# Row dot products of an expert layer on VectorE alone, without the share that GpSimd and ScalarE took

## The chip, the cores and the metric

One core of one Trainium2 chip runs one program. The metric is the device time of a run in microseconds (us), as the median of three runs. The engines are TensorE (PE for its matmuls, PEld for its weight loads), VectorE (DVE), ScalarE (ACT), GpSimd (POOL) and SyncE (SP). TensorE's granted clock is shown as a share of 2.4 GHz, so 0.50 is its lower level of 1.2 GHz.

## The reference, cut to what matters

One layer over 1024 tokens plus 16 meta tokens, width 1024: a mixer with two branches of eight heads each, and then an expert layer (`peer_ffn`) that picks 16 of 16384 experts per head and token, so 128 experts for each token:

```python
def one_block(xb):
    ...
    idx = jnp.take_along_axis(i1, ci // TOPK, axis=-1) * N_KEYS \
        + jnp.take_along_axis(i2, ci % TOPK, axis=-1)
    gate_w = jax.nn.softmax(sc, axis=-1)
    act = jax.nn.gelu(jnp.einsum('thkd,td->thk', expert_u[idx], xb).astype(jnp.float32),
                      approximate=False)
    coef = (gate_w * act).astype(xb.dtype)
    return jnp.einsum('thk,thkd->td', coef, expert_v[idx])
```

All arrays are float32. The change touches the first `einsum`: the dot product of a gathered row of `expert_u` with the token's own vector.

## The kernel before, in words

The tokens are eight blocks of 128. They go through the mixer in three groups of 2, 3 and 3 blocks (`GROUPS`, function `mixer`): projections and both branches head by head, then `branches`, `merge` and `rank` (query projection and scores), and `route`, which finds the 128 experts of each token on VectorE.

The expert layer is done in two ways. The first five blocks gather (`experts`): for each block, 128 indirect DMAs, issued on GpSimd's queue, each bring one row of `expert_u` of 1024 floats for each of the 128 tokens, 512 KB in all, into a buffer `G`. `G` has eight slots (`NG`). The list `out` holds the rows that are on their way, and `use` takes them from its head. A row of kind "u" is multiplied with the block's normalised tokens (`h2p`) and summed over the 1024 columns, which gives one column of `ac`. There are two ways to do this. Either VectorE does both in one `scalar_tensor_tensor` with `accum_out`, or GpSimd multiplies in place, the row becomes kind "a" and stays at the head of `out`, and ScalarE sums it by a copy with `accum_out`. After a block's 128 dots, 128 more gathers bring rows of `expert_v` (kind "v"), which TensorE weighs and sums in the PSUM tile `pv`. So there are 640 rows of u and 640 of v. The last three blocks go a dense way (`dense`): TensorE computes all 16384 experts for them, first with `u_t` (tile `ua`), then with `expert_v` (tile `acc`). The gathers of the first five blocks run beside the mixer of groups 1 and 2 and beside the dense part.

All instructions are put in order by a planner before the kernel is built. `Clock` keeps a planned time for each engine; `Engine` adds each instruction's estimated duration; `Weave` always takes the next piece from the generator whose planned time is earliest. The planner's estimates are 1.195 us for a fused dot on VectorE (`dve_time`: (1024 + 123) / 960), 2.28 us for the multiplication on GpSimd (`pool_time`) and 1.07 us for the sum on ScalarE (`act_time`). It has no term for two engines that hinder each other. Within an engine the order is fixed when the kernel runs. Some small choices hang on the planned clocks too: `scale` and `copy` take ScalarE or VectorE, whichever is planned to be free first, and in group 0 the split of weights (tile `wlo`) takes GpSimd or VectorE (line 397).

Which way a row's dot goes is chosen in `use`, where `DS2` is 0:

```python
if x.kind == "u" and clk.t["pool"] + 1.2 < clk.t["dve"] + DSL + max(0.0, min(DSM, DS2 * (clk.t["dve"] - clk.t["dma"]))):
    pool.tensor_tensor(x.G, x.G, x.h2, op=OP.mult)
    x.kind = "a"
    return
if x.kind == "a":
    act.activation(x.G, x.G, AF.Copy, accum_out=x.ac[:, x.j:x.j + 1])
elif x.kind == "u":
    dve.scalar_tensor_tensor(x.G, x.G, 1.0, x.h2, op0=OP.mult, op1=OP.mult,
                             accum_out=x.ac[:, x.j:x.j + 1])
```

How many rows the plan wants gathered by when is set by `bias`: in the mixers it grows when the planned DMA clock falls behind those of TensorE and VectorE, and in the dense part it ties the share of rows left to the share of weight chunks left.

Of the kernel before, what the change touches and what calls it, by code (L numbers as in the profile page):

```python
# [36 lines left out]
CB = 4  # L37
KB = 50
RW = 2
DSL = -2  # L40
PSL = 1
ASL = 0
NDENSE = 3
# [229 lines left out]
def _build(ctx, tc, nc, a, groups, dbg, peer):  # L273
# [1014 lines left out]
    def use(x):  # L1288

        if x.kind == "u" and clk.t["pool"] + 1.2 < clk.t["dve"] + DSL + max(0.0, min(DSM, DS2 * (clk.t["dve"] - clk.t["dma"]))):  # L1290
            pool.tensor_tensor(x.G, x.G, x.h2, op=OP.mult)
# [326 lines left out]
```

## Time and profile before

| what | before |
|---|---|
| median of 3 runs | 4220.03 us (4211.74 to 4225.68) |
| profiled execution, its own time | 4197.44 us |
| its span, first to last instruction | 4195.7 us |
| mean granted clock of TensorE | 0.962 |
| PE busy | 3811.1 us (91%) |
| VectorE busy | 2771.6 us (66%) |
| ScalarE busy | 1749.3 us (42%) |
| GpSimd busy | 1862.4 us (44%) |

Busy time is the time in which an engine shows an instruction; an instruction that starts and is then held up counts as busy for as long as it lasts. Shares are means over the whole span. Stage by stage: the mixer of group 0 until about 560 us, then its merge and rank; the gathers from 633 us on; the mixer of group 1 until about 1640, of group 2 until about 2780; the dense part with `u_t` until 3534, and with `expert_v` from 3553 to 4179.

### The profile page before, as it was taken

The numbers are of one execution on the slowest core, as the hardware profiler recorded it, in microseconds if no ns is written. First come the engines' busy times: TensorE is split into PE (matmuls) and PEld (weight loads), VectorE is DVE, ScalarE is ACT, GpSimd is POOL, SyncE is SP. The second block draws the span as 40 slices with busy tenths as digits, with TensorE's granted clock in tenths as the row PEclk, the third lists the DMA queues.
The fourth block names the chain that finished last, engine by engine and source line by source line (L and its number), as shares of the span: only waits on it lengthen the run. The fifth ranks groups of instructions, "written<-read, shape, count | busy, mean of one in ns | idle before, by whom it ended". The sixth has DMA issues, their size and how long they took to land. (4 is left out here: it accounts for less than half of the span.)

```text
span 4195.7 us, 62111 instructions
## 1 busy us (share of the span) xinstructions
PE 3811.1 (91%) x20086; PEld 2750.6 (66%) x20086; DVE 2771.6 (66%) x8155; ACT 1749.3 (42%) x4336; POOL 1862.4 (44%) x1633
## 2 busy tenths in 40 slices
PE   6999988998999978999999989779989898999998
PEld 5777875665445766455555557568888797766665
DVE  5555469998863658888876536669868464744444
ACT  4566443444331232344333312236648573333332
POOL 3222444445553545565656635443434243433332
PEclk9999999999999989999999999899999999999999
DMA  3332368786898988999889989888888888999996
GB/s 105 91 96 87 114 205 268 257 295 233 314 351 288 346 320 294 323 331 335 319 305 337 349 278 347 302 286 275 292 267 296 297 292 296 349 328 333 328 329 221
DMA packets 525911, 1162.17 MB, mean 277 GB/s; under 512 B 55376, under 2 KB 262000, under 8 KB 525200
## 3 DMA queue, kind: packets, MB, share of 16 engines
q0 software_dynamic: 186960, 679.04, 45.5%
q1 hardware_dynamic: 303328, 459.04, 32.9%
q10 hardware_dynamic: 35296, 20.12, 1.6%
q8 instruction: 158, 2.59, 0.3%
q14 instruction: 169, 1.38, 0.1%
HBM read 1082.32 MB, written 75.66 MB: 276 GB/s over the span
## 5 line engine op out<-in xcount | busy, mean ns | idle before, releaser
L185 POOL DMA_INDIRECT G<-in_expert_v_dram,idxT x640 | 737.0, 1152 | 1070.6 <-PE pv L185 482.1
L185 POOL DMA_INDIRECT G<-in_expert_u_dram,idx x640 | 724.5, 1132 | 733.2 <-DVE G L185 247.1
L185 DVE TENSOR_TENSOR wlo<-wraw,whi 128x512 fp32r<-128x512 f32 (+2 forms) x644 | 543.8, 851 | 725.2 <-ACT whi L185 688.5
L185 ACT CAST whi<-wraw 128x512 fp32r<-128x512 f32 (+2 forms) x816 | 527.6, 659 | 577.7 <-PE prj L185 201.6
L185 DVE SCALAR_TENSOR_TENSOR G<-G,h2p 128x1024 f32<-128x1024 f32 x574 | 710.6, 1241 | 11.2 <-DMA G<-in_expert_u_dram,idx 11.2
L185 PE MATMUL ua<-hD,whi 128*128 128x384 f32 x2048 | 542.1, 346 | 31.7 <-ACT whi L185 31.6
L185 PE MATMUL prj<-hW,wraw 128*128 128x384 f32 x1280 | 476.3, 506 | 18.4 <-ACT junk L185 7.2
L185 PEld LDWEIGHTS ua<-hD,whi 128*128 128x128 f32 x2048 | 367.7, 191 | 70.5 <-ACT whi L185 36.8
L185 POOL TENSOR_TENSOR wlo<-wraw,whi 128x384 fp32r<-128x384 f32 (+1 forms) x172 | 202.6, 1186 | 401.0 <-ACT whi L185 344.5
L185 PE MATMUL prj<-wraw,hW 128*128 128x512 f32 x768 | 378.0, 606 | 0.0
L185 PE MATMUL pv<-G,Zb 128*32 128x512 f32 x2560 | 365.0, 621 | 14.1 <-DMA G<-in_expert_v_dram,idxT 14.0
L185 PE MATMUL ua<-hD,wlo 128*128 128x384 f32 x1024 | 350.4, 342 | 10.9 <-DVE wlo L185 9.9
L185 PEld LDWEIGHTS prj<-hW,wraw 128*128 128x128 f32 x1280 | 234.8, 197 | 165.0 <-issue 29.0
L185 PE MATMUL acc<-whi,Chi 128*128 128x512 f32 x768 | 309.3, 403 | 17.3 <-ACT whi L185 17.0
L185 PE MATMUL acc<-wlo,Chi 128*128 128x512 f32 x768 | 300.0, 391 | 0.5 <-DVE wlo L185 0.5
L185 PE MATMUL acc<-whi,Clo 128*128 128x512 f32 x768 | 300.0, 391 | 0.0
L185 PEld LDWEIGHTS acc<-whi,Chi 128*128 128x128 f32 x768 | 144.4, 188 | 110.8 <-issue 63.7
L185 PEld LDWEIGHTS ua<-hD,wlo 128*128 128x128 f32 x1024 | 195.0, 190 | 17.2 <-DVE wlo L185 17.0
L185 PE MATMUL prj<-oTs,whi 128*128 128x384 f32 (+1 forms) x768 | 186.3, 330 | 19.0 <-DVE oTs L185 9.8
L185 PEld LDWEIGHTS prj<-wraw,hW 128*128 128x128 f32 x768 | 131.1, 194 | 90.1 <-issue 84.8
L185 ACT CAST Chi<-Gr 128x384 fp32r<-128x384 f32 x125 | 64.1, 513 | 264.6 <-DVE Gr L185 211.2
L185 PEld LDWEIGHTS acc<-whi,Clo 128*128 128x128 f32 x768 | 144.5, 188 | 31.5 <-DVE Clo L185 0.3
(326 smaller groups left out, 7241.1 us busy)
## 6 DMA issues: line engine op xcount, KB each, us to landing
wraw<-in_u_t_dram SPq DMA_DIRECT2D x256, 256.0 KB, 4.8
wraw<-in_expert_v_dram SPq DMA_DIRECT2D x128, 512.0 KB, 5.4
wraw<-in_w_b_dram SPq DMA_DIRECT2D x192, 256.0 KB, 4.8
wraw<-in_w_a_dram SPq DMA_DIRECT2D x192, 192.0 KB, 3.9
wraw<-in_w_q_dram SPq DMA_DIRECT2D x96, 256.0 KB, 5.9
gscr<-Gl SPq DMA_DIRECT2D x125, 192.0 KB, 4.7
Gr<-gscr SPq DMA_DIRECT2D x125, 192.0 KB
wraw<-in_w_g_dram SPq DMA_DIRECT2D x96, 192.0 KB, 6.0
```

What stands on the lines that cost most here:

```text
L185: return f(*a, **k)
```

## The change

One constant in the rule of `use` changes. With -2 the GpSimd way is taken when GpSimd's planned clock lies more than 3.2 us behind VectorE's; with -1000 it would have to lie more than 1001.2 us behind.

```diff
@@ -37,7 +37,7 @@
 CB = 4
 KB = 50
 RW = 2
-DSL = -2
+DSL = -1000
 PSL = 1
 ASL = 0
 NDENSE = 3
```

## Rows read from the trace of the kernel before

**Rows 1.** The page, part 1: busy time of each engine over the span.

```profile
PE 3811.1 (91%) x20086; PEld 2750.6 (66%) x20086; DVE 2771.6 (66%) x8155; ACT 1749.3 (42%) x4336; POOL 1862.4 (44%) x1633
```

**Rows 2.** Windows: length; busy of PE, PEld, DVE, ACT, POOL; clock; DMA share; GB/s.

```profile
633.00:3670.00 3037.00, 2755.51 (x14069) 1929.33 (x14068) 2175.04 (x6600) 1252.73 (x3096) 1479.18 (x1241) 0.96 0.87 305
633.00:1050.00 417.00, 379.45 (x1708) 237.24 (x1707) 376.21 (x1217) 177.94 (x538) 202.25 (x164) 0.96 0.78 263
1420.00:1640.00 220.00, 178.38 (x929) 140.15 (x930) 147.01 (x361) 69.48 (x122) 109.74 (x89) 0.90 0.89 317
2460.00:2790.00 330.00, 273.54 (x1405) 208.59 (x1404) 203.71 (x508) 92.03 (x158) 160.25 (x139) 0.91 0.88 309
3670.00:4196.00 526.00, 508.48 (x2431) 352.74 (x2429) 244.17 (x433) 157.27 (x204) 165.83 (x150) 0.99 0.89 308
...
3700.00:4100.00 400.00, 399.68 (x1917) 276.03 (x1916) 190.66 (x340) 125.23 (x163) 140.04 (x127) 1.00 0.95 328
```

**Rows 3.** The chain that ended last, from 4130 us: start, length, what.

```profile
4134.93 7.90 DMA G<-in_expert_v_dram,idxT
...
4143.94 33.60 PE acc L185 x147
```

**Rows 4.** Tile G: count, min/median/max ns of one, first and last start.

```profile
L185 POOL DMA_INDIRECT G<-in_expert_u_dram,idx x640: 932/940/4291, 633.0 to 3640.6; - x160
...
L185 DVE SCALAR_TENSOR_TENSOR G<-G,h2p x574: 1154/1218/14726, 644.2 to 3654.4; 128x1024 f32<-128x1024 f32 x192
L185 DVE DVE_READ_ACCUMULATOR G<-G,h2p x574: 70/83/97, 645.4 to 3655.6; 128x1 f32 x192
L185 POOL TENSOR_TENSOR G<-G,h2p x66: 2327/2374/2704, 645.0 to 3660.6; 128x1024 f32<-128x1024 f32 x66
L185 ACT ACTIVATE G<-G x66: 1040/1056/1080, 647.7 to 3665.1; 128x1024 f32<-128x1024 f32 x66
L185 ACT ACTIVATION_READ_ACCUMULATOR G<-G x66: 182/187/215, 648.7 to 3666.1; 128x1 f32 x66
```

**Rows 5.** VectorE's timeline near 645, 982 and 3662 us.

```profile
645.38 2.77 DVE L185 TENSOR_TENSOR hit<-iota_c,posf 128x400 f32<-128x400 f32 x1
648.18 0.58 DVE L185 TENSOR_TENSOR hit<-hit,cand 128x400 f32<-128x400 f32 x1
...
981.93 14.73 DVE L185 SCALAR_TENSOR_TENSOR G<-G,h2p 128x1024 f32<-128x1024 f32 x1
...
3661.62 2.46 DVE L185 TENSOR_TENSOR wlo<-wraw,whi 128x1024 fp32r<-128x1024 f32 x1 [3.11 <-ACT whi L185]
...
3667.23 1.23 DVE L185 TENSOR_TENSOR wlo<-wraw,whi 128x1024 fp32r<-128x1024 f32 x1 [1.44 <-ACT whi L185]
```

**Rows 6.** GpSimd's timeline near 982 us.

```profile
981.74 13.83 POOL L185 TENSOR_TENSOR G<-G,h2p 128x1024 f32<-128x1024 f32 x6
```

**Rows 7.** TensorE's timeline near 982 us; in brackets the idle time before it.

```profile
997.38 0.79 PE L185 MATMUL bg<-vtok,Y 128*128 128x128 f32 x2 [12.51 <-ACT X L185]
```

**Rows 8.** Windows over 42 held-up VectorE instructions, each to 2 us past it; their sum.

```profile
sum 197.00, PE 149.54 PEld 114.19 DVE 181.39 ACT 97.63 POOL 122.49; mean PE 3.56 PEld 2.72 DVE 4.32 ACT 2.32 POOL 2.92
```

**Rows 9.** Windows, columns as in Rows 2: a stretch full of fused dots, and after 989.7 us.

```profile
941.00:981.00 40.00, 38.53 (x184) 23.78 (x183) 37.42 (x129) 18.09 (x55) 24.61 (x19) 1.00 0.82 271
...
989.70:1003.40 13.70, 6.02 (x11) 3.54 (x12) 13.32 (x41) 4.51 (x10) 6.49 (x4) 0.50 0.23 72
```

**Rows 10.** Tile h2p from 633 to 1050 us, columns as in Rows 4.

```profile
L185 DVE SCALAR_TENSOR_TENSOR G<-G,h2p x122: 1201/1217/14726, 644.2 to 1048.7; 128x1024 f32<-128x1024 f32 x122
...
L185 POOL TENSOR_TENSOR G<-G,h2p x14: 2327/2354/2704, 645.0 to 993.2; 128x1024 f32<-128x1024 f32 x14
```

**Rows 11.** Waits of all engines: us in total, times, longest.

```profile
POOL G L185 <- ACT G L185: 352.7, 53, 44.4
```

**Rows 12.** Waits of TensorE's matmuls, columns as in Rows 11.

```profile
PE pv L185 <- DMA G<-in_expert_v_dram,idxT: 14.0, 11, 2.7
```

**Rows 13.** Windows of tile idxT: VectorE, GpSimd (gathers of v); clock, DMA, GB/s.

```profile
3670.00:4196.00 526.00, 0.29 (x1) 159.16 (x138) 0.99 0.89 308
```

## The prediction

> **What bounds the kernel now.** I read the busy times first. TensorE is busy for 3811.1 of 4195.7 us, no other engine for more than 66% [rows 1], and the work that ended last is a run of 147 matmuls of the dense part, with two output blocks behind it [rows 3]. The change alters no matmul. So the time can move only by the 384.6 us in which TensorE is idle, by stretches in which it is granted its lower clock, and by whatever would make the last stage wait.
>
> Next I asked where this idle time lies. The 66 rows that go the GpSimd way fall between 645 and 3661 us [rows 4], and in 633 to 3670 TensorE is idle for 3037 - 2755.5 = 281.5 us [rows 2]. In the last stretch that is full of gathers, 3700 to 4100, it is idle for 0.3 us [rows 2]: there is nothing to win there, and only something to lose.
>
> Then I looked at what VectorE does while GpSimd multiplies. From 981.74 us GpSimd runs six multiplications in 13.83 us [rows 6]. A fused dot of VectorE that started 0.19 us after them took 14.73 us [rows 5], where 1.218 us is usual [rows 4]. It came out as GpSimd was done. The same is seen with others: a comparison of 128x400 took 2.77 us beside the multiplication at 645.0, and its neighbour of that size 0.58 us; a weight split took 2.46 us beside the last multiplication, and the next one 1.23 us [rows 5]. In all, 42 VectorE instructions that overlap one of the 66 multiplications last over 0.5 us longer than the median of their own form (the pairs shown are the first and the last of these 42). Their surplus adds up to 99.9 us. So a multiplication on GpSimd doesn't take work off VectorE here: it holds VectorE up for 99.9 / 66 = 1.51 us on average, and a fused dot with its accumulator read would cost 1.218 + 0.083 = 1.30 us [rows 4].
>
> TensorE feels it. In the windows over these 42 instructions it is idle for 197.0 - 149.5 = 47.5 us [rows 8], 24% of them; elsewhere in 633 to 3670 it is idle for (281.5 - 47.5) / (3037 - 197) = 8.2%. Beyond that share, 47.5 - 0.082 x 197 = 31.3 us of idle time lie beside held-up instructions. The largest piece is the 12.51 us before 997.38, which ends as the fused dot comes free and ScalarE and TensorE get their input [rows 7].
>
> **The change, part by part.** All sums are against the profiled execution's 4197.4 us.
>
> *Multiplications removed from GpSimd.* 66 x 2.374 = 157 us of GpSimd go. GpSimd's own time is not on the path (44% busy [rows 1]); what counts is VectorE's 99.9 us of hold-up. What is that worth to TensorE? At least the one gap whose cause can be followed instruction by instruction, 12.5 us; at most the whole surplus, 31.3 us. Some of the rest would be there anyway, because the planner takes the GpSimd way just when VectorE is late. I take the middle, -22.
>
> *Clock.* After the long gap TensorE worked at half its clock from 989.7 to 1003.4 us, with 6.0 us of matmuls in it [rows 9], which would take 3.0 at the full clock. The other gaps beside the held-up instructions are under 5 us. Between 0 and -6; I take -4.
>
> *Fused dots added to VectorE.* 66 x 1.30 = 86 us, against 99.9 us that go: VectorE's busy time should fall by some 14 us. The price for TensorE lies between nothing and the rate that the hold-ups show, 31.3 / 99.9 = 0.31 us for each us of delay, so 27 us. The nearest row is a stretch where VectorE is 94% busy, mostly with fused dots: 941 to 981, where TensorE is idle for 1.5 of 40 us [rows 9], 3.7%. A dot of 1.3 us fits between the planned uses; a hold-up of 2.7 us less often does. 0.037 x 86 = 3; I take +3 and keep 27 for the range.
>
> *Sums removed from ScalarE.* 66 x (1.056 + 0.187) = 82 us of 1749 [rows 1, 4]. It is 42% busy, so nothing to -5; I take 0.
>
> *Gathers.* GpSimd stands for 352.7 us before gathers whose slot ScalarE's sum frees [rows 11], and these waits go; others of the same kind behind VectorE's dots take part of their place. TensorE, however, waits for gathered rows for only 14.0 us in all [rows 12]: 0 to -14, and I take -3.
>
> By a rule of the Trainium skill the price would be larger. The page "SBUF — State Buffer", section "Who interferes with whom", says that a VectorE instruction with two SBUF inputs and a GpSimd instruction that reads SBUF exclude each other, and that whichever comes second waits until the first is done. If every multiplication met such an instruction, VectorE would lose 66 x 2.374 = 157 us instead of 99.9, and the gain from the hold-up would be 157 / 99.9 of mine, -35 instead of -22. The trace decides: some multiplications meet nothing that they hold up.
>
> *The order.* The planner counts 1.195 us more on VectorE for each of the 66 rows, 79 us in all, 0 on GpSimd and ScalarE, and will weave everything after 645 us differently; `scale` and `copy` will take ScalarE somewhat more often. What such a reshuffle can do is seen from the two tails of the mixer, which do the same work for three blocks: 220 - 178.4 = 41.6 us idle in one, 330 - 273.5 = 56.5 in the other [rows 2]. I take 0, with 15 us to either side.
>
> Sum: -22 - 4 + 3 + 0 - 3 + 0 = -26 us, so 4171 for a profiled execution like this one. That execution lies 22.6 us under the median of the runs, 4220.0. I take the same difference from the median: 4194 us, 0.6% faster. About 0.3%, 12.7 us, is what a measurement of this kernel can tell from no change.
>
> **The rivals.**
>
> *Nothing to measure.* If TensorE's idle time beside the hold-ups was there for other reasons, only the long gap and its clock come back, -12.5 - 3; and if the dots cost half of their upper rate, 13 us go again: -2.5, so 4217. For it: the multiplications stand where VectorE is late by plan, which means stage changes, where TensorE has gaps anyway. Against it: 24% idle beside 8.2%.
>
> *Too much left for the end (slower).* If the dots are planned 79 us later, rows slip by 79 / (3037 / 640) = 17, and as v follows u, 17 of u and 17 of v move past 3670 us, where 138 rows of v are gathered now [rows 13]. A row is 0.524 MB, at 328 GB/s [rows 2] 1.6 us. DMA is 95% busy in 3700 to 4100, which leaves 20 us: enough for 13 rows. 34 rows would need 54 us, so TensorE would wait for 34 us: 4254. It decides from 13 rows on. Against it: in the mixers the plan's bias calls rows by DMA's lag, and DMA rather than VectorE is nearly full there, 0.88 to 0.89 in the tails [rows 2].
>
> *A full engine gets fuller (slower).* From 633 to 1050 VectorE is busy for 376 of 417 us [rows 2], and 14 of the 66 rows lie there [rows 10]. If VectorE's queue sets that stretch's end, 14 x 1.30 = 18 us are added, and if the hold-ups there fell into time that it had, nothing comes back: 4238. The Trainium skill, "Perfetto Trace Analysis", section "Optimizing Scalar/DVE Operations", says that with a saturated VectorE it may pay to move work to other engines, GpSimd too; the same paragraph warns that these two share a read port. Against it: 13.5 us of the stretch are the one held-up dot itself, more than half of the 18.
>
> That the change does nothing can be ruled out: GpSimd's planned clock would have to lie 1001 us behind VectorE's, but each gather moves it on, and the gathers wait for slots that VectorE frees.
>
> **How the numbers follow.** Forecast (-26; its own range -13 to -45, so 4175 to 4207) 0.5; nothing to measure 0.3; too much left 0.12; fuller engine 0.08. The forecast splits into 0.45 faster and 0.05 within 0.3%; the second case 0.05 faster, 0.24 same and 0.01 slower; the last two 0.02 same and 0.18 slower. Together 0.50, 0.31, 0.19. The low end takes all the terms' best: -31 - 6 + 0 - 5 - 14 - 15 = -71, about 4150. The high end must take in most of the slower cases: 4242.
>
> **What would show it.** Right: 640 fused dots near 1.22 us and none of over 3; no multiplication of `G` on GpSimd; VectorE busy for some 14 us less, ScalarE for 82 less and GpSimd for about 157 less; no gap of TensorE like that before 997; TensorE's idle time in 633 to 3670 down from 281 to about 255. Wrong: idle time of TensorE after 3670 us, with rows of u there; or VectorE over 95% busy in the stretch after 633 with TensorE's idle time up. If the idle time beside the hold-ups is gone and the total is the same, the order took it back elsewhere.

## The result and the profile after

The changed kernel takes 4165.9 us (4151.5 to 4172.0, four runs) against 4222.0 us for the kernel before beside it: a ratio of 0.9872, 95% interval 0.9848 to 0.9896. Timed once more, with the last experiments, it gave 0.9878 (0.9860 to 0.9895). So it is 1.2 to 1.3% faster, some 51 to 54 us. The forecast was 4194 us, 0.6% or 26 us faster, with a range of 4150 to 4242: the direction holds and the range holds the time, but the gain is twice the forecast.

A reading aid for all that follows: the trace of before that the prediction rests on came from an execution that ran 22.6 us under its median. A second trace of the same kernel, taken with the first experiment, has a span of 4209.7 us. Where times are compared, the ratios to before on the same chip are used, and a difference of ratios is turned into us with 4210. The experiments ran on three chips, and after itself ran again on only one of them, with the last four; "slower than after" takes its ratio there, 0.9878, for all, and each such difference has some 10 us to either side.

The page of the changed kernel, part 1, busy time of each engine over its span of 4170.3 us:

```profile
PE 3808.9 (91%) x20086; PEld 2761.5 (66%) x20086; DVE 2746.6 (66%) x8282; ACT 1684.7 (40%) x4209; POOL 1720.4 (41%) x1567
```

Against [rows 1], VectorE has 25 us less, ScalarE 65, GpSimd 142. VectorE does 66 more dots and is busy for less time. ScalarE's fall is less than the 82 us of its sums.

Its tile `G`, count, min/median/max ns, first and last start, and the same windows as in [rows 2] (length; busy of PE, PEld, DVE, ACT, POOL; clock; DMA share; GB/s):

```profile
L185 DVE SCALAR_TENSOR_TENSOR G<-G,h2p x640: 1199/1218/1285, 646.0 to 3632.3; 128x1024 f32<-128x1024 f32 x160
L185 DVE DVE_READ_ACCUMULATOR G<-G,h2p x640: 70/83/93, 647.1 to 3633.4; 128x1 f32 x160
```

```profile
633.00:3670.00 3037.00, 2776.38 (x14168) 1953.75 (x14167) 2159.48 (x6746) 1194.31 (x2976) 1319.77 (x1183) 0.96 0.88 308
633.00:1050.00 417.00, 388.15 (x1742) 240.55 (x1740) 370.79 (x1278) 165.85 (x517) 181.82 (x157) 0.97 0.83 274
...
3700.00:4100.00 400.00, 400.00 (x1919) 276.30 (x1919) 193.07 (x341) 125.90 (x162) 161.46 (x122) 1.00 0.96 333
```

All 640 dots are on VectorE, at the same median as in [rows 4], and the longest takes 1.285 us instead of 14.7. TensorE is idle for 3037 - 2776.4 = 260.6 us in 633 to 3670, where it was 281.5 [rows 2], or 288.8 in the second trace of before. In 633 to 1050 it is idle for 28.9 us instead of 37.6. In 3700 to 4100 it is not idle at all.

The waits for slots have moved, not gone. In the waits of all engines (us in total, times, longest), the row of ScalarE in [rows 11] is missing. The row of VectorE in before, and those of VectorE and TensorE in after, are:

```profile
POOL G L185 <- DVE G L185: 450.6, 167, 41.6
```

```profile
POOL G L185 <- DVE G L185: 708.0, 184, 44.4
POOL G L185 <- PE pv L185: 591.0, 183, 56.6
```

In before GpSimd stood for 450.6 us behind VectorE's dots and for 352.7 behind ScalarE's sums, 803 in all; now it is 708 behind the dots alone. What a large wait is worth can't be read from its own size.

### The profile page after: what moved, and what is told of

The parts are those of the page before. It is cut to its first block, busy times and chain, and to the rows that moved or that the text cites. A ratio compares the mean times of both kernels' runs of the same rounds, so it can differ in the third digit from the quotient of the medians.

```text
span 4170.3 us, 62056 instructions
## 1 busy us (share of the span) xinstructions
PE 3808.9 (91%) x20086; PEld 2761.5 (66%) x20086; DVE 2746.6 (66%) x8282; ACT 1684.7 (40%) x4209; POOL 1720.4 (41%) x1567
## 5 line engine op out<-in xcount | busy, mean ns | idle before, releaser
L185 POOL DMA_INDIRECT G<-in_expert_v_dram,idxT x640 | 755.2, 1180 | 1128.7 <-PE pv L185 536.4
L185 DVE TENSOR_TENSOR wlo<-wraw,whi 128x512 fp32r<-128x512 f32 (+2 forms) x644 | 513.3, 803 | 720.3 <-ACT whi L185 666.7
L185 DVE SCALAR_TENSOR_TENSOR G<-G,h2p 128x1024 f32<-128x1024 f32 x640 | 776.6, 1217 | 14.3 <-DMA G<-in_expert_u_dram,idx 12.9
L185 PEld LDWEIGHTS prj<-oTs,whi 128*128 128x128 f32 x768 | 137.8, 198 | 40.1 <-issue 11.9
```

The lines of the kernel that those rows point to most:

```text
L185: return f(*a, **k)
```

## The experiments

The question was which part of the change gives the gain: that GpSimd's multiplications no longer hold VectorE up, that GpSimd's queue is shorter, that ScalarE is free of the sums, or only that the planner wove another order. Each ratio below is to before on the same chip, with its 95% interval.

**Before once more.**

```diff
(no edit)
```

> The kernel before, unchanged, timed against itself and traced a second time. Every theory expects a ratio within 0.3% of 1. The question is what one trace of this kernel is worth: the first trace of before ran 22 us under its median, and the two traces differ by 25 us where the runs differ by 56. If the trace shows a span near 4220 us, the missing 30 us will be seen in its stages; the 12.5 us gap of TensorE before 997 us should stand in it again if it belongs to the order of the instructions.

Measured: 1.0006 (0.9989 to 1.0023), so the comparison can see some 0.2%. The gap is there again. TensorE's and VectorE's timelines of this trace:

```profile
995.61 0.79 PE L185 MATMUL bg<-vtok,Y 128*128 128x128 f32 x2 [12.44 <-ACT X L185]
```

```profile
980.23 14.66 DVE L185 SCALAR_TENSOR_TENSOR G<-G,h2p 128x1024 f32<-128x1024 f32 x1
```

The held-up dot lasts 14.66 us and the gap 12.44, where the first trace has 14.73 and 12.51 [rows 5, 7]. In this trace 45 instructions beside the 66 multiplications are held up, by 111.4 us (42 and 99.9 in the first). The hold-ups repeat; they are no accident of one execution.

**Before's order, dots on VectorE.** The planner is told what it was told in before; the instructions that come out differ.

```diff
 if x.kind == "u" and clk.t["pool"] + 1.2 < ...:
+    pool.swap = lambda *a, **k: nc.vector.scalar_tensor_tensor(
+        x.G, x.G, 1.0, x.h2, op0=OP.mult, op1=OP.mult, accum_out=x.ac[:, x.j:x.j + 1])
     pool.tensor_tensor(x.G, x.G, x.h2, op=OP.mult)
+    pool.swap = None
...
 if x.kind == "a":
+    act.swap = lambda *a, **k: None
     act.activation(x.G, x.G, AF.Copy, accum_out=x.ac[:, x.j:x.j + 1])
+    act.swap = None
```

> The planner sees before's program, so the order on TensorE is that of before, instruction by instruction; only the 66 multiplications on GpSimd and the 66 sums on ScalarE are left out, and 66 fused dots stand on VectorE at the places of the multiplications. Hold-up theory (GpSimd's multiplications held VectorE up): most of the gain comes without a new order, 30 to 56 us faster than before, ratio 0.987 to 0.993. Order theory (the gain is the new order that the planner wove): within 0.3% of before, or slower by the 86 us of dots times up to 0.31, ratio 0.997 to 1.006.

Measured: 0.9904 (0.9878 to 0.9931), 40 us faster, 29 to 51. TensorE runs the same instructions in the same order as in before. No VectorE instruction beside a gathered row is held up any more, and the gap before 997 us is gone, although the six dots that replace the six multiplications stand on VectorE there. The window of 633 to 3670:

```profile
633.00:3670.00 3037.00, 2782.72 (x14232) 1946.58 (x14232) 2167.30 (x6760) 1199.59 (x2977) 1329.85 (x1185) 0.96 0.88 309
```

TensorE is idle for 254.3 us here. The order theory falls as an account of the whole: most of the gain comes without a new order. The run takes three things away at once, the hold-up, GpSimd's time and ScalarE's sums, and adds the dots; the runs after it add one thing at a time.

Three more rows of this trace: the waits of GpSimd and of TensorE's matmuls, and the stretch where the matmuls now stand that had the gap before them in before.

```profile
POOL G L185 <- DVE G L1291: 350.0, 43, 46.9
PE pv L185 <- DMA G<-in_expert_v_dram,idxT: 14.2, 11, 2.5
```

```profile
975.00:989.00 14.00, 12.63 (x53) 8.20 (x52) 13.59 (x61) 5.12 (x15) 0.00 (x0) 1.00 0.51 168
```

The gathers wait behind the moved dots (L1291) for as long as they did behind ScalarE's sums, 350.0 us where it was 352.7 [rows 11], and the kernel is 40 us faster: the gain doesn't come from shorter waits for slots. TensorE's wait for gathered rows hasn't changed either, 14.2 us and 14.0 [rows 12], though 157 us of GpSimd's time are gone. And TensorE has its full clock in that stretch.

As the order is the same, this trace and the second one of before can be laid beside each other matmul by matmul. From 633 to 1123 us, where 16 of the 66 rows lie and 29 us of hold-up go, this one gains 17 us; from 1692 to 2927, with 18 rows and 23 us of hold-up, it gains 1; from 2927 to 3215, with 12 rows and 23 us, 11. (Against the first trace of before it is 20, 0 and 11; the two traces of before differ from each other by up to 8 us in a single stretch.) So what the exchange is worth depends on the place. Why it is worth nothing in the middle isn't shown.

**GpSimd's multiplications put back as extra work.** After's program; the 66 rows are the ones that before gave to GpSimd (`AT` lists them by block and number, here and in the runs below). The row's buffer is dead at this point, so this adds nothing to the result.

```diff
 elif x.kind == "u":
     dve.scalar_tensor_tensor(x.G, x.G, 1.0, x.h2, ...)
+    if (x.b, x.j) in AT:
+        nc.gpsimd.tensor_tensor(x.G, x.G, x.h2, op=OP.mult)
```

> After's program and order, and behind the dots of the same 66 rows as in before GpSimd multiplies the row's buffer, which nobody reads any more, with the tokens (66 times 2.4 us of GpSimd that add nothing to the result). Hold-up theory: VectorE is held up by about 1.5 us for each, 100 us in all, and the time goes back by 20 to 45 us, ratio to before 0.992 to 0.998; VectorE's instructions of more than twice their usual time are back in the trace. Order theory: 0.987, as after, since the order is after's.

Measured: 1.0050 (1.0032 to 1.0067): not only the gain goes, it is slower than before. Against after that is 72 us for 66 multiplications, more than the 20 to 45 expected. 56 VectorE instructions are held up, by 113.9 us. VectorE's and GpSimd's timelines near 1520 us:

```profile
1520.14 3.48 DVE L186 TENSOR_TENSOR wlo<-wraw,whi 128x512 fp32r<-128x512 f32 x1 [0.28 <-ACT whi L186]
1523.54 1.21 DVE L186 SCALAR_TENSOR_TENSOR G<-G,h2p 128x1024 f32<-128x1024 f32 x1
```

```profile
1520.68 2.38 POOL L1301 TENSOR_TENSOR G<-G,h2p 128x1024 f32<-128x1024 f32 x1
1523.21 1.24 POOL L186 DMA_INDIRECT G<-in_expert_u_dram,idx  x1 [0.16 <-issue]
```

A weight split that takes 0.69 us elsewhere takes 3.48: by these rows it starts half a microsecond before the multiplication, and ends half a microsecond after it.

**Memsets in place of the multiplications.**

```diff
+    if (x.b, x.j) in AT:
+        for n in range(3):
+            nc.gpsimd.memset(x.G[:, :900], 0.0)
```

> As the run with the added multiplications, at the same 66 places, with three memsets of 900 columns in place of each, about as long on GpSimd but reading nothing (the values that they leave are not used). If it is reading by GpSimd that holds VectorE up: as after, ratio to before 0.985 to 0.990, and no held-up instruction. If it is GpSimd's time or its later gathers that cost: the same as with the added multiplications, 0.992 to 0.998.

Measured: 0.9955 (0.9939 to 0.9971), 32 us slower than after: within the range given for GpSimd's time or its later gathers. But the run doesn't part the two theories, for the hold-ups are not gone; they are of another kind. VectorE's and GpSimd's timelines near 3093 us:

```profile
3092.94 2.08 DVE L186 TENSOR_SCALAR e<-iota_c,iT 128x128 f32<-128x128 f32 x4
3094.94 0.67 DVE L186 TENSOR_TENSOR wlo<-wraw,whi 128x512 fp32r<-128x512 f32 x1
```

```profile
3093.08 2.72 POOL L1302 MEMSET G<- 128x900 f32 x3 [3.17 <-DVE G L186]
```

Four scalar operations that take 1.11 us elsewhere in this trace take 2.08 beside the memsets; the weight split, with its two inputs in SBUF, starts inside the last memset and takes its usual 0.67. Over the run 45 instructions are held up, by 31.6 us: 43 scalar operations, a copy and a cast, none with two inputs. (The expectation of a later run says 46 and 33; one of those was no such instruction.) Beside the multiplications of the run before it was 35 with two inputs and 21 with one.

**Short memsets.** GpSimd's time in pieces that hold nothing up for long. With the gaps between them, the twenty memsets take 3.21 us at each place and 216 us in all; the added multiplication took 2.40, 164 in all, and the three long memsets 2.68, 177 in all.

```diff
+    if (x.b, x.j) in AT:
+        for n in range(20):
+            nc.gpsimd.memset(x.G[:, :8], 0.0)
```

> After's program, with 20 memsets of 8 columns on GpSimd behind the dot of the same 66 rows: about as long on GpSimd as a multiplication, but each of about 0.1 us, so that no instruction of VectorE can be held up for long. In the run with memsets of 900 columns 46 VectorE instructions were held up by 33 us in all, all with one SBUF input (scalar multiplications, copies, casts), none with two. If hold-up is what costs: as after, ratio 0.986 to 0.990. If GpSimd's time before the next gather costs by itself: as with the long memsets, 0.994 to 0.997.

Measured: 0.9934 (0.9912 to 0.9956), 24 us slower than after (12 to 35), without one instruction held up beside them. So work added to GpSimd costs something besides hold-up. Two waits of this run, TensorE's for gathered rows and GpSimd's before the memsets (us, times, longest):

```profile
PE pv L186 <- DMA G<-in_expert_v_dram,idxT: 25.1, 14, 4.5
POOL G L1302 <- DVE G L186: 126.8, 36, 21.9
```

TensorE's wait was 11.0 us in after, so here gathers that GpSimd issues later let TensorE wait for rows; in the runs with multiplications and with long memsets it is only 15.7 and 15.5. The second row is a rival to GpSimd's time: a memset waits for the dot in front of it, and the gathers behind it in GpSimd's queue wait with it. In before GpSimd was idle for only 1.2 us in all before its 66 multiplications. Which share of the 24 us is GpSimd's time and which this standing is not told apart; memsets over another tile, which wait for no dot, would tell. How much of it was in before is not shown.

**Extra dots on VectorE.** The sum goes into `spare`, a tile of one column that nobody reads.

```diff
+    if (x.b, x.j) in AT:
+        nc.vector.scalar_tensor_tensor(x.G, x.G, 1.0, x.h2, op0=OP.mult, op1=OP.mult, accum_out=spare)
```

> After's program, with a second fused dot on VectorE behind that of the same 66 rows, into the row's dead buffer: 66 times 1.30 us, 86 us more on VectorE, in an unchanged order. Prediction's term (a dot fits between planned uses, 0.037 us for each us): 3 us more than after, ratio to before 0.986 to 0.990. If each us on VectorE costs what a held-up us cost in the runs with GpSimd work added (some 60 us for 115): 35 to 55 us more, ratio 0.995 to 1.001.

Measured: 0.9946 (0.9928 to 0.9963), 29 us slower than after (18 to 39) for 86 us of VectorE, 0.33 us for each. The prediction's 3 us falls; its upper bound of 27 was about right.

**Extra sums on ScalarE, over the row and over another tile.**

```diff
+    if (x.b, x.j) in AT:
+        nc.scalar.activation(x.G, x.G, AF.Copy, accum_out=spare)               # first run
+        nc.scalar.activation(junks[D][0], x.h2, AF.Copy, accum_out=spare)      # second run
```

> After's program, with a copy with sum on ScalarE behind the dot of the same 66 rows, over the row's dead buffer: 82 us more on ScalarE, and the buffer's slot is freed by ScalarE, as it was in before. Hold-up theory: hardly anything, 0 to 10 us more than after, ratio to before 0.986 to 0.991. Slot theory (before lost its time because gathers waited for ScalarE's sums): 15 to 40 us more, ratio 0.991 to 0.997, with GpSimd standing before gathers for some hundred us behind ScalarE again.

> After's program with the same 66 copies with sum on ScalarE, but over the tokens' tile into a spare tile, so that ScalarE waits for no dot and no slot waits for ScalarE. In the run where the copies read the row, ScalarE stood for 130 us behind VectorE's dots. If ScalarE's time itself costs (82 us): as that run, ratio to before 0.997 to 1.001. If it was its waiting in the middle of its queue: near after, 0.987 to 0.992, and the sums, which the planner of before had placed with care, were no large part of before's loss.

Measured: 0.9994 (0.9977 to 1.0011) over the row, 0.9902 (0.9885 to 0.9919) over the other tile. The first lies above both of its forecasts, the second where waiting was expected to be the cost. The same work costs 49 us in one place and 10 in the other, and the 10 are at the edge of what can be told from none. In the first run's waits of all engines ScalarE stands behind the dots, and gathers behind ScalarE:

```profile
POOL G L186 <- ACT G L1302: 148.5, 35, 22.1
...
ACT G L1302 <- DVE G L186: 130.0, 55, 8.7
```

A sum in the middle of ScalarE's queue that must wait for VectorE, 130.0 us in all here, stops what stands behind it. In before, ScalarE waited for only 26 us for GpSimd's products, since the planner had given these sums a place. The 49 us are therefore no measure of what the sums cost in before; 10 us is the nearer one. Which share the held slots have in the 49 and which ScalarE's standing is not told apart.

**The weight splits on VectorE too, and other orders.** The planner's other rule for GpSimd is switched off, or its cost for a dot is set to what the trace shows, or both.

```diff
-PSL = 1
+PSL = -1000
...
-    return (free(x) + (123 if "scalar_tensor" in name else 65)) / 960.0
+    return (free(x) + (223 if "scalar_tensor" in name and free(x) == D else 123 if "scalar_tensor" in name else 65)) / 960.0
```

> After's program, with the planner's other rule for GpSimd off too (PSL -1000): the 172 weight splits of group 0 that GpSimd took go to VectorE, so that GpSimd computes on no large tile at all. The trace of after holds 60 us of held-up VectorE instructions before 640 us. Hold-up theory: these 60 us go, VectorE gets 172 splits of 0.55 to 0.69 us, 105 us, in a stretch where it is busy for half the time; 0 to 15 us faster than after, ratio to before 0.983 to 0.988. Load theory (VectorE's own time counts as much as a hold-up): 10 to 30 us slower than after, ratio 0.990 to 0.995.

> After's program from a planner that counts 1.299 us instead of 1.195 for a VectorE instruction with a scalar and 1024 columns, which is what the trace shows for a fused dot with its accumulator read. All work is the same; only the order differs from after's. This shows what a new order alone does: if it is noise, a ratio to before within 0.5% of after's 0.987, so 0.982 to 0.992; if the truer cost lets the planner do better, 0.980 to 0.985.

> Both together: the weight splits of group 0 on VectorE too (0.986 alone) and the truer cost of the dot. A candidate to beat both kernels: 0.978 to 0.985 if the two add up, 0.985 to 0.990 if the order swallows it.

> After unchanged, on the same chip as these three, with its interval: 0.985 to 0.990. Against the run with before's order and the dots on VectorE (0.990): if the new order has a part of its own, after lies clearly under 0.9878; if not, within 0.988 to 0.992.

Measured: splits 0.9863 (0.9835 to 0.9892), dot cost 0.9887 (0.9870 to 0.9904), both 0.9860 (0.9839 to 0.9881), after itself 0.9878. None can be told from after: the best is 8 us ahead of it on the same chip, with intervals that overlap. That the splits alone take the 60 us of hold-ups before 640 us away is seen in the trace, where no instruction of VectorE is held up any more; but 172 splits are VectorE's then, and nothing measurable is left.

## Why the prediction was half right

**What bounds the kernel, and the hold-up.** Right. The trace showed that VectorE pays for GpSimd's multiplications, and the runs confirm it from both sides: take them away in the same order, with the sums, and 40 us go though the dots are added; put them into after's order and 72 come.

**The price of the hold-up.** Mis-sized. I priced 99.9 us of hold-up at -22, at most -31, by TensorE's idle time in windows that end 2 us past each held-up instruction. Adding multiplications and adding short memsets differ by 1.0050 - 0.9934 = 1.16%, 49 us (37 to 61, from both intervals), for 113.9 us of hold-up: 0.43 us for each. The multiplications and the long memsets, on one chip and with about the same time on GpSimd, differ by 1.0050 - 0.9955 = 0.95%, 40 us (30 to 50), for 113.9 - 31.6 = 82 us of hold-up: 0.49. At 0.43, 99.9 us cost 43. So on average a late VectorE instruction costs TensorE more than the gap right beside it, as the rows of before could not show. It is an average: in before's order the exchange between 1692 and 2927 us was worth next to nothing. The -35 that the prediction works out by assuming 157 us of hold-up comes nearer to 43 only by chance, since the hold-up was 99.9 and 111.4 us in the two traces.

**Clock.** Right for the gap. In before's order the eleven matmuls behind it take 3.1 us less, where 3.0 was worked out and -4 taken. Not all other gaps beside held-up instructions are under 5 us: one of 6.1 us ends at 1528, but it is there without the hold-up too (5.5). What the clock did elsewhere is not told apart, since TensorE's busy time differs by 17.5 us between two traces of after itself (3808.9 and 3791.4).

**GpSimd's time and the gathers.** Open. "GpSimd's own time is not on the path (44% busy)" was too quick: work added to GpSimd without hold-up cost 24 us, by its time or by its standing behind the dots. But for before the row that the term went by didn't move when the multiplications went (14.0 and 14.2 us), so -3 of 0 to -14 is not refuted there. That waits behind dots take the place of those behind sums was right. A mean of 44% says little about a queue whose next item is a gather that someone will wait for.

**The fused dots.** Mis-sized the other way, and by most: +29 instead of +3. I took the 3.7% idle time of one stretch full of dots as their price. That stretch shows how much TensorE idles while VectorE computes dots; it doesn't show whether the work queued behind them comes late. The upper bound, 0.31 us for each us, was nearly the measured 0.33.

**ScalarE's sums.** Taken as 0, bound -5; about -10 (0 to -20).

**The sum.** -43 for the hold-up with its clock, 0 to -24 for GpSimd's time, -10 for ScalarE, +29 for the dots: -24 to -48, where the run in before's order gave -40 (-29 to -51) and after gave -51 to -54. The terms come from additions to another order, so they don't settle how the 40 us divide. The error of the dots (+26) and those of the hold-up with its clock (-17) and of ScalarE (-10) nearly cancel. That a forecast with these wrong sizes was off by no more than half is luck.

**The order.** Taken as 0, and still open. Its 15 us rested on two tails "which do the same work", but the two windows hold 929 and 1405 matmuls [rows 2]. After (0.9878 and 0.9872) and before's order with the dots moved (0.9904) differ by 0.3%, less than the intervals allow to tell. Another order of the same work (0.9887) is as fast as after.

**The rivals.** "Nothing to measure" falls with the result. "Too much left for the end" needed 13 more rows in the tail; the window of tile `idxT` after 3670 us shows 130 gathers where [rows 13] has 138, and TensorE is never idle in 3700 to 4100.

```profile
3670.00:4171.00 501.00, 0.29 (x1) 174.96 (x130) 0.99 0.89 307
```

"A full engine gets fuller" falls as well: in 633 to 1050 VectorE is busy for 370.8 us with 138 dots, where it was 376.2 with 122 [rows 2, 10].

**What would show it.** As said: the dots' durations, no multiplication, the gap gone, TensorE's idle time at 260.6 where about 255 was expected (245.4 in the second trace of after), VectorE down (25 us, not 14), GpSimd down by 142 of 157. ScalarE fell by 65 of 82, and by 64 in before's order too (1685.2 us busy), where nothing else on it changes: the 82 us add up durations that overlap each other and their neighbours, and without the sums ScalarE would be busy for 1683.0 us in the trace of before, 66 less.

## What to carry to other kernels

Before work is given to an engine with free time, look in the trace at what the other engine does meanwhile: an instruction that lasts several times its median beside one particular partner is being held up, and the share of busy time hides that. Price an engine's time by adding a known amount of it to the kernel, at the same places and in the same order, and not by the idle time next to it; 86 us more on an engine that is 66% busy cost 29 here. Let what you add wait for nothing: the same sums cost 49 us where they waited in the middle of an in-order queue, and 10 where they didn't. And where two kernels have the same order, lay their traces beside each other: it shows where the time was won.

## What the runs showed of the hardware

Which VectorE instructions GpSimd holds up depends on what GpSimd does. Beside multiplications, 35 of the 56 held-up instructions read two operands from SBUF and 21 read one; beside memsets of 0.85 us all 45 were scalar operations, copies or casts with one operand, and the 171 instructions with two that overlap a memset took at most 0.08 us longer than usual. The Trainium skill states this on the page "SBUF — State Buffer", section "Who interferes with whom": two SBUF inputs conflict with a GpSimd instruction that reads SBUF and not with one that only writes, while copies, casts and scalar operations can run in a mode that conflicts with either. The trace agrees, with 0 of 45 and 35 of 56. That whichever comes second waits, as the prediction puts it, the trace doesn't bear out: by the start times of the profile, which are rough for GpSimd, 21 of the 42 held-up instructions in before started up to 0.66 us before the multiplication, and still ended after it.

A held-up instruction can wait through several partners in a row: six multiplications of 2.3 us, issued one after another, kept one dot for 14.7 us, and again for 14.66 in the second trace. It did not get in between two of them.
